# Value stage: left operands listed one product earlier, four buffers for V's outputs, block stores begun by ScalarE, one tile's scaling on GpSimd

## The chip, the cores and the metric

The kernel runs on one core of one Trainium2 chip. The metric is device time in microseconds (us) of one execution, from three executions of the kernel, of which the median is taken; a fourth execution was run under the profiler, and every row of the profile comes from that one. Engines carry the profile's names: PE is TensorE (matmul), DVE is VectorE, ACT is ScalarE, POOL is GpSimd and SP is SyncE, which in this kernel only begins DMA transfers.

## The reference

The computation is a two-layer trunk over 2048 rows of 1024 channels. The first layer is a chunked gMLP mixer; the second is banded attention that reads a K and a V computed once from the rows after the first layer. What matters here is the V half of that shared projection:

```python
def rms_norm(x, g):
    xf = x.astype(jnp.float32)
    y = xf * lax.rsqrt(jnp.mean(xf * xf, axis=-1, keepdims=True) + EPS)
    return (y * g.astype(jnp.float32)).astype(x.dtype)

def shared_kv(x, g_kv, w_kv):
    bsz, s, _ = x.shape
    k, v = jnp.split(rms_norm(x, g_kv) @ w_kv, 2, axis=-1)
...
    x = x + gmlp_mixer(...)                     # layer A
    k_pad, v_pad = shared_kv(x, kv_norm_g, w_kv)
    h = rms_norm(x, b_norm_g[i])
    x = x + chunk_attention_mixer(h, k_pad, v_pad, b_w_qz[i], b_rel_bias[i], b_w_out[i])
    return rms_norm(x, final_norm_g)
```

All of it is float32. The kernel writes each float32 operand of a matmul as the sum of a high part (a cast to the type fp32r) and a low part (the operand less its high part), and forms a product as hi·hi + hi·lo + lo·hi: three matmuls instead of one.

## The kernel before, in words

**Stages.** Layer A runs until about 1347 us of the span. Then comes the *Value stage* (to about 1520 us), which computes V for all 2048 rows, and then, tile by tile, the projections to K, Q and Z (tile names `pj`, `raw_b`, `wh_b`, `wl_b`), attention (`s`, `tp`, `pv`) and the output projection.

**The Value stage.** It takes the rows in four tiles t = 0 to 3 of 512 rows, each four blocks b = 0 to 3 of 128 rows. The V product of a tile (512x1024 by 1024x1024) is done by Strassen's scheme with seven half-size products, taken in the order ph = 1, 7, 2, 6, 5, 4, 3 (`PHS`), each for two halves of the rows, jp = 0, 1. I write (ph,jp) for one of these fourteen products of a tile. A product is twelve matmuls into one PSUM tile: for each k = 0 to 3 one hi·hi (L111), one high left by low weight (L112), one low left by high weight (L113). Three kinds of work stand around the matmuls:

- *Left operands* (`v_left`, L1257 to L1280). For each product ACT casts a 128x512 part of the normalised rows to its high part `Shv` (L337) and DVE subtracts it for the low part `Slv` (L342). Then, in place, POOL forms the sums of Strassen's scheme: after ph = 1 `a11 -= a21` (L1273) and `a21 += a22` (L1274), after ph = 7 `a11 = a22 - a11` (L1276), after ph = 2 `a12 -= a11` (L1278). Block buffers of even tiles are named `bx_b`, those of odd tiles `xo_b`; blocks 0 and 1 hold the operands of jp = 0, blocks 2 and 3 those of jp = 1. PE's L113 of a product waits for its `Slv`.
- *Eviction* (`v_evict`, L1288 to L1326). DVE combines the products (L1314, L1317, L1319, L1322, L1325), POOL adds two of them (L1320), and a finished 128x512 part of V is split again into a buffer `v` by ACT (L1296) and DVE (L1297), and stored to DRAM by SP (L1301, `vhd<-v`). The buffers `v` are two.
- *Next tile's rows.* While tile t is multiplied, `norm(t+1,b)` loads a block (L141), sums its squares on ACT (L143), adds epsilon on DVE (L125), raises to -1/2 on POOL (L126, `rr_b`) and scales the block on DVE (L148). `block(t+1,b)` then transposes it on PE (L162, eight 128x128 transposes into two PSUM banks of four), ACT copies the result back (two L168), and SP stores it to DRAM for later (L169, `xtd<-xo_b` or `xtd<-bx_b`). POOL's sums overwrite the block in place, so the first of them must wait for that store to have landed.

In tile 0 the weights of the later products are split as well (ACT L228, DVE L229: `vwh`, `vwl`), because they are loaded there for the first time.

**What sets the order.** `strassen()` (L296) is a generator: it writes out the matmuls of a product, yields four times per product, and asks for the left operands of a later product (`ready`) and for weights (`weigh`) after the second k. The loop over tiles (L1336 on) uses the yields, numbered i = 0 to 55 in a tile, to write out `norm` and `block` of the next tile (for t = 0 from i = 30 and i = 45 every 3; otherwise from i = 1 every 3 and i = 20 every 8). The framework's scheduler then gives every engine its list, near to that written order; an engine works through its list strictly in order and waits on semaphores. What is written earlier is therefore ahead in the list of each engine it touches.

Of the kernel before, what the change touches and what calls it, by code (L numbers as in the profile page):

```python
# [10 lines left out]
F32R = mybir.dt.float32r  # L11
BF16 = mybir.dt.bfloat16
AF = mybir.ActivationFunctionType
ALU = mybir.AluOpType
# [3 lines left out]
P = 128  # L18
# [4 lines left out]
NT = S // T  # L23
# [10 lines left out]
def trunk_kernel(  # L34
# [19 lines left out]
    nc = tc.nc  # L54
# [84 lines left out]
    def norm(t, b, junk):  # L139
        xt = xf[t, b] = place[0](t, b)  # L140
        nc.sync.dma_start(xt[:], x1d[t][b * P : (b + 1) * P, :])  # L141
        r = sm.tile([P, 1], F32, tag="rr", name=f"rr_b{t}_{b}", bufs=4)
        on_tick(nc.scalar.activation(  # L143
            junk(f"jk_b{t}_{b}")[:].bitcast(BF16), xt[:], AF.Square, scale=1.0 / 32,
            accum_out=r[:],
        ))
        root(r[:])
        nc.vector.tensor_scalar(xt[:], xt[:], r[:], None, op0=ALU.mult)  # L148

    def x_tiles():  # L150
        th = sh.tile([P, KD, T], F32R, tag="hh", name="hh_b")
# [3 lines left out]
    def block(t, b):  # L155
        xt = xf[t, b]
        half = [
            banks[0].tile([P, 4, P], F32, tag="t4", name=f"tr_b{t}_{b}_{h}", bufs=4)
            for h in range(2)
        ]  # L160
        for k in range(KD):
            ins = tpose(half[k // 4][:, k % 4, :], xt[:, k * P : (k + 1) * P], ident[:])  # L162
            if k == 0:
                on_tick(ins)
        x3 = xt[:].rearrange("p (k c) -> p k c", k=KD)
        for h in range(2):
            ks = slice(h * 4, h * 4 + 4)
            nc.scalar.copy(x3[:, ks, :], half[h][:])  # L168
        nc.sync.dma_start(xtd[t][:, b, :], xt[:])  # L169

    x_place = []

# [118 lines left out]

    PHS = (1, 7, 2, 6, 5, 4, 3)

    def strassen(name, right, left, evict, look):

        todo = [(ph, jp) for ph in PHS for jp in range(2)]  # L296
        rts, views = {}, {}

        def weigh(n):
            for ph in PHS[:n]:  # L300
                if ph not in rts:
                    rts[ph] = right(ph)

        def ready(i):
            if i < len(todo):
                views[i] = left(*todo[i])

        ready(0)
        if not look:
            yield  # L310
        weigh(1)
        deep = look == 2
        if deep:
            ready(1)
        for i, (ph, jp) in enumerate(todo):
            ps = pmm.tile([P, 512], F32, tag="mm", name=f"{name}_{ph}_{jp}")
            vs = views.pop(i)
            for k in range(4):
                hi, lo = rts[ph][k // 2]
                c = slice((k % 2) * 512, (k % 2) * 512 + 512)  # L320
                ins = mm3(ps[:], *vs[k], hi[:, c], lo[:, c], k == 0, k == 3)
                tick.append(ins.ins.name)
                if k == 1:
                    weigh(i // 2 + (2 if jp else 1 + look))
                    ready(i + 1 + deep)
                if k < 3:
                    yield
            evict(ph, jp, ps[:])
            yield
# [54 lines left out]
    with ExitStack() as actx:  # L384
# [624 lines left out]
        for n in range(2, 6):  # L1009
            b = start[n, 1]  # L1010
# [219 lines left out]
    with ExitStack() as vctx:  # L1230
        def v_pool(name):
            return vctx.enter_context(tc.tile_pool(name=name, bufs=1, reuse_waits="tile"))

        def v_weights(pool, ph):
            for q in range(2):
                vw[ph, q] = [pool.tile([P, 1024], F32R, name=f"vw{i}{ph}_{q}")[:] for i in "hl"]

        vpw, vps, vpx, vpc, vpu, vpv, vpy, vp2, vpt = (
            v_pool(n) for n in ("vpw", "vps", "vpx", "vpc", "vpu", "vpv", "vpy", "vp2", "vpt")
        )  # L1240
        for ph in (4, 3):
            v_weights(vpw, ph)
# [45 lines left out]
        def v_evict(t):  # L1288
            xa, ya = {}, {}

            def out(r, c, jp, y):
                v = vpv.tile([P, 4, 256], F32R, tag="v", name=f"v{t}_{r}{c}{jp}", bufs=2)
                o4 = y.rearrange("p (a b c) -> p a b c", a=4, b=2)
                for hd in range(2):
                    h = v[:, :, hd * 192 : hd * 192 + 64]
                    nc.scalar.copy(h, o4[:, :, hd, :])  # L1296
# [4 lines left out]
                nc.sync.dma_start(  # L1301
                    vhd[t][:, 4 * c : 4 * c + 4, 2 * jp + r, :], v[:].bitcast(F32)
                )
# [28 lines left out]
        )  # L1332
        pieces = []
        vsplit = []
        for t in range(NT):
            for i, _ in enumerate(  # L1336
                strassen(f"vp{t}", v_right(t), v_left(t), v_evict(t), 1 if t else 2)
            ):
                n0, b0 = (30, 45) if t == 0 else (1, 20)
                dn, db = (3, 3) if t == 0 else (3, 8)  # L1340
                if i and i % 4 == 0 and vsplit:
# [18 lines left out]

# [705 lines left out]
```

## Time and profile before

| what | before |
|---|---|
| median of 3 executions | 2645.97 us (2645.60 to 2647.23) |
| profiled execution: time / span | 2649.25 us / 2647.5 us (1.75 us lie around the span) |
| mean granted PE clock | 0.997 |
| busy: PE, DVE, ACT, POOL | 98%, 71%, 49%, 34% |
| PE waits in the stretch 1340 to 1530 us, by the table of waits | 8.1 us in 9 waits |

How to read it: PE is busy in all but 2% of the span and works strictly in order, so time is lost only where PE waits, and a wait taken out there moves everything behind it forward. The table of waits lists, for one engine, the line it waited at, the engine and line that released it, the sum, how often and the longest. In the timeline each row is a start, a duration, the engine, the line, the operation with out<-in names, and in brackets the idle time before it and what ended that; `x2` marks neighbouring like rows put together. SP's rows are the issue of a transfer, not the transfer itself; the view of one tile gives the time from issue to landing.

### The profile page before, as it was taken

How to read it: one execution, taken by the hardware profiler on the slowest of the kernel's cores; microseconds unless marked ns; L12 is line 12 of the kernel's file. 1: busy time of each engine (PE TensorE's matmuls, PEld its weight loads, DVE VectorE, ACT ScalarE, POOL GpSimd, SP SyncE). 2: the span in 40 equal slices, each digit the busy share in tenths (PEclk: the TensorE clock that was granted, in tenths of full speed). 3: DMA queues.
4: the chain of work that ended last, by engine and by line, in shares of the span. 5: the costliest groups of instructions: out<-in, count | busy, mean ns of one | idle time of the engine just before them, and what ended most of it. 6: DMA issues, size and time to landing. Idle time of an engine off the chain costs nothing. (4 is left out here: it accounts for less than half of the span.)

```text
span 2647.5 us, 38028 instructions
## 1 busy us (share of the span) xinstructions
PE 2607.3 (98%) x12976; PEld 2179.8 (82%) x12976; DVE 1889.1 (71%) x2946; ACT 1303.1 (49%) x2303; POOL 893.7 (34%) x874
## 2 busy tenths in 40 slices
PE   8999999999999999999999999999999999999997
PEld 7888888888888888888878778888888888888886
DVE  6655676766767668757777767778778777877677
ACT  5422243443433434343356456666666655666564
POOL 4611335143152322203234434344332232332245
PEclk9999999999999999999999999999999999999999
DMA  7898998989988868967776587778787666875666
GB/s 291 313 347 331 345 367 321 315 324 340 335 318 294 311 235 328 328 201 270 282 266 209 194 284 229 233 240 264 251 269 258 224 208 220 256 229 159 195 227 249
DMA packets 273857, 718.74 MB, mean 271 GB/s; under 512 B 28800, under 2 KB 68736, under 8 KB 273664
## 3 DMA queue, kind: packets, MB, share of 16 engines
q1 hardware_dynamic: 273664, 716.31, 78.2%
q8 instruction: 104, 1.70, 0.3%
q14 instruction: 89, 0.73, 0.1%
HBM read 531.12 MB, written 174.59 MB: 267 GB/s over the span
## 5 line engine op out<-in xcount | busy, mean ns | idle before, releaser
L111 PE MATMUL P<-T,S 128*128 128x512 f32 x1248 | 495.7, 397 | 0.0
L113 PE MATMUL P<-T,S 128*128 128x512 f32 x1248 | 488.1, 391 | 0.1
L112 PE MATMUL P<-T,S 128*128 128x512 f32 x1248 | 487.8, 391 | 0.2 <-DVE T L444 0.2
L1488 POOL TENSOR_SCALAR pr<-pr,sl 128x640 f32<-128x640 f32 (+4 forms) x256 | 206.9, 808 | 553.9 <-DVE sl L1487 467.4
L111 PE MATMUL pj<-hh_b,wh_b 128*128 128x512 f32 x768 | 319.9, 417 | 0.7 <-ACT wh_b L228 0.7
L113 PE MATMUL pj<-hh_b,wl_b 128*128 128x512 f32 x768 | 304.2, 396 | 0.8 <-DVE wl_b L229 0.7
L112 PE MATMUL pj<-hl_b,wh_b 128*128 128x512 f32 x768 | 302.9, 394 | 0.1
L1484 ACT ACTIVATE pr<-pr,nm 128x640 f32<-128x640 f32 (+4 forms) x256 | 195.5, 764 | 186.2 <-DVE nm L1477 184.8
L113 PEld LDWEIGHTS P<-T,S 128*128 128x128 f32 x1248 | 234.6, 188 | 50.9 <-DVE S L444 0.4
L112 PEld LDWEIGHTS P<-T,S 128*128 128x128 f32 x1248 | 235.3, 189 | 45.3 <-DVE T L444 0.6
L111 PEld LDWEIGHTS P<-T,S 128*128 128x128 f32 x1248 | 235.2, 188 | 44.8 <-DVE x L577 0.4
L1509 DVE TENSOR_TENSOR pt<-tp,pt 128x640 fp32r<-128x640 f32 (+4 forms) x256 | 188.5, 736 | 43.8 <-ACT pt L1508 41.2
L1477 DVE CUSTOM_DVE_ANT_0 pr<-s,bias 128x640 f32<-128x640 f32 (+4 forms) x256 | 188.1, 735 | 32.5 <-PE s L1469 27.2
L1508 ACT CAST pt<-tp 128x640 fp32r<-128x640 f32 (+4 forms) x256 | 159.0, 621 | 54.1 <-PE tp L1504 49.7
L1504 PE MATMUL tp<-ident,pr 128*128 128x128 f32 x1120 | 166.5, 274 | 9.6 <-DVE pt L1509 7.8
L113 PEld LDWEIGHTS pj<-hh_b,wl_b 128*128 128x128 f32 x768 | 144.4, 188 | 35.7 <-DVE wl_b L229 2.9
L1504 PEld LDWEIGHTS tp<-ident,pr 128*128 128x128 f32 x1120 | 130.6, 140 | 44.3 <-issue 14.6
L111 PEld LDWEIGHTS pj<-hh_b,wh_b 128*128 128x128 f32 x768 | 145.3, 189 | 18.8 <-ACT wh_b L228 2.4
L1529 PEld LDWEIGHTS pv<-pt,V 128*128 128x128 f32 x896 | 143.0, 188 | 20.2 <-DVE pt L1509 3.2
L112 PEld LDWEIGHTS pj<-hl_b,wh_b 128*128 128x128 f32 x768 | 145.3, 189 | 16.9 <-DVE hl_b L186 0.5
L1529 PE MATMUL pv<-pt,V 128*128 128x256 f32 (+3 forms) x896 | 153.9, 319 | 1.9 <-ACT pt L1508 1.0
L229 DVE TENSOR_TENSOR wl_b<-raw_b,wh_b 128x1024 fp32r<-128x1024 f32 x96 | 120.2, 1253 | 28.2 <-ACT wh_b L228 27.0
(302 smaller groups left out, 5732.7 us busy)
## 6 DMA issues: line engine op xcount, KB each, us to landing
S<-hsd SPq DMA_DIRECT2D x288, 512.0 KB, 5.5
rw<-in_w_a SPq DMA_DIRECT2D x108, 512.0 KB, 6.5
A<-ytd SPq DMA_DIRECT2D x72, 512.0 KB, 5.8
raw_b<-wk SPq DMA_DIRECT2D x72, 512.0 KB, 4.3
hsd<-S SPq DMA_DIRECT2D x56, 512.0 KB, 4.7
V<-vhd SPq DMA_DIRECT2D x56, 512.0 KB, 5.6
bias<-reld SPq DMA_DIRECT2D x64, 320.0 KB, 3.9
va<-vd SPq DMA_DIRECT2D x32, 512.0 KB, 6.0
```

Of the source, the lines that this page charges most:

```text
L111: first = mm(ps, lh, rh, start=first, stop=False)
L112: mm(ps, lh, rl, start=False, stop=False)
L113: mm(ps, ll, rh, start=False, stop=last)
L229: tv(wl[:], raw[:], wh[:].bitcast(F32), op=sub)
L1477: nc.vector.tensor_tensor_reduce(out=pr[:, c0:].rearrange("p (a b) -> p a b", a=nseg), in0=ps[:, :nseg, :w], in1=bias[:, c0:].rearrange("p ...
L1484: nc.scalar.activation(pr[:, c0:], pr[:, c0:], AF.Exp, scale=-1.0, bias=nm[:], accum_out=sl[:])
L1488: nc.gpsimd.tensor_scalar(pr[:, c0:], pr[:, c0:], sl[:], 1.0, op0=ALU.mult, op1=ALU.mult)
L1504: ins = tpose(tp[:, b, :], pr[:, b * P : (b + 1) * P], ident[:])
L1508: nc.scalar.copy(oh, tp[:, b0:5, :].rearrange("p a b -> p (a b)"))
L1509: nc.vector.tensor_tensor(pt[:, 2560 + o + b0 * P : 2560 + o + 640], tp[:, b0:5, :].rearrange("p a b -> p (a b)"), oh.bitcast(F32), op=ALU ...
L1529: mm(po[:, q0 * P : q1 * P], vtl[t, p][:, i, hs], rhs, start=(i == blocks[0] and j == 0), stop=(i == 7 and j == 1),)
```

## The change

It has four parts.

1. *Left operands listed further ahead.* `strassen()` takes `deep`, and lists the operands of `deep` + 1 products before the first matmul, and then always of the product `deep` + 1 ahead: three ahead in tile 0 (was two), two ahead in tiles 1 to 3 (was one). The generators of all tiles are made beforehand, and the next tile's is started at i = 54 of the current tile, so that the operands of its first products are listed before the current tile's last eviction.
2. *Four buffers for V's outputs.* The parts of V with c = 1 (`v_010`, `v_011`, `v_110`, `v_111`) get a pool of their own, `vpz`, with two buffers; those with c = 0 keep `vpv`.
3. *Block stores begun by ScalarE.* `xtd<-xo_b` and `xtd<-bx_b` go from SP's list to ACT's.
4. *One scaling on GpSimd.* `norm` of tile 1 (which runs during tile 0) scales its four blocks on POOL instead of DVE.

The diff:

```diff
@@ norm
-        nc.vector.tensor_scalar(xt[:], xt[:], r[:], None, op0=ALU.mult)
+        if t == 1:
+            nc.gpsimd.tensor_scalar(xt[:], xt[:], r[:], 1.0, op0=ALU.mult, op1=ALU.mult)
+        else:
+            nc.vector.tensor_scalar(xt[:], xt[:], r[:], None, op0=ALU.mult)
@@ block
-        nc.sync.dma_start(xtd[t][:, b, :], xt[:])
+        nc.scalar.dma_start(xtd[t][:, b, :], xt[:])
@@ strassen
-    def strassen(name, right, left, evict, look):
+    def strassen(name, right, left, evict, look, deep=0):
...
         ready(0)
-        if not look:
+        for i in range(deep):
+            ready(i + 1)
+        if deep or not look:
             yield
         weigh(1)
-        deep = look == 2
-        if deep:
-            ready(1)
         for i, (ph, jp) in enumerate(todo):
...
                     ready(i + 1 + deep)
@@ v_evict
-                v = vpv.tile([P, 4, 256], F32R, tag="v", name=f"v{t}_{r}{c}{jp}", bufs=2)
+                pool = vpz if c else vpv
+                v = pool.tile([P, 4, 256], F32R, tag="v", name=f"v{t}_{r}{c}{jp}", bufs=2)
@@ the loop over tiles
+        tiles = [
+            strassen(f"vp{t}", v_right(t), v_left(t), v_evict(t), 1 if t else 2, 1 if t else 2)
+            for t in range(NT)
+        ]
+        next(tiles[0])
         for t in range(NT):
-            for i, _ in enumerate(
-                strassen(f"vp{t}", v_right(t), v_left(t), v_evict(t), 1 if t else 2)
-            ):
+            for i, _ in enumerate(tiles[t]):
...
+                if i == 54 and t + 1 < NT:
+                    next(tiles[t + 1])
```

Added lines shift the line numbers a little: in the changed kernel `Slv` is L344, POOL's four sums are L1276, L1277, L1279 and L1281, the evictions L1318 to L1329, DVE's scaling L151 and POOL's L149, the block store L172.

PE's list is the same but for one group of transposes that moves by one matmul, and the lists of DVE and POOL in tiles 2 and 3 are unchanged. The instructions move at three places.

**DVE in tile 0, from the split of the first weights of ph = 4 on** (`vw` are weights, `Slv_4_0` is the left operand of product (4,0), `rr_b_0` and `xo_b_0` belong to block 0 of tile 1). Before:

```order
L229 TENSOR_TENSOR vwl_0_11952<-st_0_12142,vwh_0_11951 128x1024
L125 TENSOR_SCALAR rr_b_0_12176<-rr_b_0_12176 128x1
L1319 TENSOR_TENSOR vu_1_1_12017<-vp_6_1_12158,vu_1_1_12017 128x512
L148 TENSOR_SCALAR xo_b_0_12174<-xo_b_0_12174,rr_b_0_12176 128x1024
L229 TENSOR_TENSOR vwl_1_11954<-st_1_12144,vwh_1_11953 128x1024
L342 TENSOR_TENSOR Slv_4_0_12201<-bx_b_1_11687,Shv_4_0_12200 128x512
L125 TENSOR_SCALAR rr_b_1_12206<-rr_b_1_12206 128x1
```

and now:

```order
L232 TENSOR_TENSOR vwl_0_11955<-st_0_12149,vwh_0_11954 128x1024
L344 TENSOR_TENSOR Slv_4_0_12175<-bx_b_1_11687,Shv_4_0_12174 128x512
L125 TENSOR_SCALAR rr_b_0_12183<-rr_b_0_12183 128x1
L1323 TENSOR_TENSOR vu_1_1_12025<-vp_6_1_12165,vu_1_1_12025 128x512
L232 TENSOR_TENSOR vwl_1_11957<-st_1_12151,vwh_1_11956 128x1024
L344 TENSOR_TENSOR Slv_4_1_12208<-bx_b_3_11828,Shv_4_1_12207 128x512
L125 TENSOR_SCALAR rr_b_1_12213<-rr_b_1_12213 128x1
```

`Slv_4_0` now stands right behind the first weight split, four rows earlier; the scaling L148 is gone from DVE's list, and `Slv_4_1` has come up to where `rr_b_1` was.

**POOL at the turn from tile 0 to tile 1** (`xo_b` are tile 1's blocks, `rr_b_0_12434`, now `rr_b_0_12442`, and `rr_b_1` the norm of tile 2). Before:

```order
L1273 TENSOR_TENSOR xo_b_0_12174<-xo_b_0_12174,xo_b_1_12204 128x512
L1276 TENSOR_TENSOR xo_b_0_12174<-xo_b_1_12204,xo_b_0_12174 128x512
L1274 TENSOR_TENSOR xo_b_1_12204<-xo_b_1_12204 128x512
L126 TENSOR_TENSOR rr_b_0_12434<-rr_b_0_12434,mhalf 128x1
L126 TENSOR_TENSOR rr_b_1_12454<-rr_b_1_12454,mhalf 128x1
L1273 TENSOR_TENSOR xo_b_2_12233<-xo_b_2_12233,xo_b_3_12263 128x512
L1274 TENSOR_TENSOR xo_b_3_12263<-xo_b_3_12263 128x512
```

and now:

```order
L1276 TENSOR_TENSOR xo_b_0_12181<-xo_b_0_12181,xo_b_1_12211 128x512
L1277 TENSOR_TENSOR xo_b_1_12211<-xo_b_1_12211 128x512
L1276 TENSOR_TENSOR xo_b_2_12240<-xo_b_2_12240,xo_b_3_12270 128x512
L1279 TENSOR_TENSOR xo_b_0_12181<-xo_b_1_12211,xo_b_0_12181 128x512
L1277 TENSOR_TENSOR xo_b_3_12270<-xo_b_3_12270 128x512
L126 TENSOR_TENSOR rr_b_0_12442<-rr_b_0_12442,mhalf 128x1
L126 TENSOR_TENSOR rr_b_1_12462<-rr_b_1_12462,mhalf 128x1
```

The sums on blocks 2 and 3, which need the stores of these two blocks, have moved ahead of the two powers of tile 2's norm.

**DVE at the same turn**, from the first norm of tile 2 on. Before, with `Slv_7_1` (the left operand of tile 1's fourth product) as the last row:

```order
L125 TENSOR_SCALAR rr_b_0_12434<-rr_b_0_12434 128x1
L148 TENSOR_SCALAR bx_b_0_12432<-bx_b_0_12432,rr_b_0_12434 128x1024
L1297 TENSOR_TENSOR v_011_12407<-vu_1_1_12017,v_011_12407 128x4x64 x2
L125 TENSOR_SCALAR rr_b_1_12454<-rr_b_1_12454 128x1
L148 TENSOR_SCALAR bx_b_1_12452<-bx_b_1_12452,rr_b_1_12454 128x1024
L342 TENSOR_TENSOR Slv_7_1_12492<-xo_b_2_12233,Shv_7_1_12491 128x512
L342 TENSOR_TENSOR Slv_2_0_12520<-xo_b_0_12174,Shv_2_0_12519 128x512
L342 TENSOR_TENSOR Slv_2_1_12540<-xo_b_2_12233,Shv_2_1_12539 128x512
```

and now:

```order
L125 TENSOR_SCALAR rr_b_0_12442<-rr_b_0_12442 128x1
L151 TENSOR_SCALAR bx_b_0_12440<-bx_b_0_12440,rr_b_0_12442 128x1024
L125 TENSOR_SCALAR rr_b_1_12462<-rr_b_1_12462 128x1
L151 TENSOR_SCALAR bx_b_1_12460<-bx_b_1_12460,rr_b_1_12462 128x1024
L344 TENSOR_TENSOR Slv_7_1_12472<-xo_b_2_12240,Shv_7_1_12471 128x512
L125 TENSOR_SCALAR rr_b_2_12486<-rr_b_2_12486 128x1
L151 TENSOR_SCALAR bx_b_2_12484<-bx_b_2_12484,rr_b_2_12486 128x1024
L344 TENSOR_TENSOR Slv_2_0_12500<-xo_b_0_12181,Shv_2_0_12499 128x512
```

`Slv_7_1` has the two scalings of tile 2 ahead of it in both lists, and now the scaling of block 2 stands ahead of `Slv_2_0` as well. On ACT the stores of blocks 2 and 3 (L172) stand, in this order, behind the copies of block 2 and the cast `Shv_1_1`, and behind the first cast of `v_011`, tile 0's last output.

Two smaller moves concern transfers: SP's load of the raw weight `raw_b_2_1` of the projection (L246), which stood ahead of the first stores of `Qh`, now stands behind the load `V_1` of attention, and the load `raw_b_2_0` behind it.

More of the change, by code (lines that the diff above doesn't have):

```diff
@@ L1236, in v_weights @@
                 vw[ph, q] = [pool.tile([P, 1024], F32R, name=f"vw{i}{ph}_{q}")[:] for i in "hl"]
-        vpw, vps, vpx, vpc, vpu, vpv, vpy, vp2, vpt = (
-            v_pool(n) for n in ("vpw", "vps", "vpx", "vpc", "vpu", "vpv", "vpy", "vp2", "vpt")
+        vpw, vps, vpx, vpc, vpu, vpv, vpy, vp2, vpt, vpz = (
+            v_pool(n)
+            for n in ("vpw", "vps", "vpx", "vpc", "vpu", "vpv", "vpy", "vp2", "vpt", "vpz")
         )
```

## The prediction

> **What bounds the kernel now.** I read the table of PE's waits over the Value stage first, then PE's own timeline at each wait, then the engine that released it.
>
> ```profile
> engine line waited for: us in total, times, longest us
> PE vp L113 <- DVE Slv L342: 5.2, 5, 1.7
> PE vp L113 <- DVE rr_b L125: 1.4, 1, 1.4
> PE pj L111 <- ACT wh_b L228: 0.7, 1, 0.7
> PE pj L113 <- DVE wl_b L229: 0.5, 1, 0.5
> PE vp L111 <- ACT Shv L337: 0.3, 1, 0.3
> ```
>
> PE is the bound, and all that a change in this stage can win is the 8.1 us of these nine waits and the restarts behind them. PE's rows put them in four places:
>
> ```profile
> 1370.79 0.39 PE L111 MATMUL vp<-vwh,Shv 128*128 128x512 f32 x1
> ...
> 1373.51 0.39 PE L111 MATMUL vp<-vwh,Shv 128*128 128x512 f32 x1
> ...
> 1376.93 0.50 PE L113 MATMUL vp<-vwh,Slv 128*128 128x512 f32 x1 [1.45 <-DVE rr_b L125]
> ...
> 1379.56 0.39 PE L112 MATMUL vp<-vwl,Shv 128*128 128x512 f32 x1
> 1381.48 0.50 PE L113 MATMUL vp<-vwh,Slv 128*128 128x512 f32 x1 [1.53 <-DVE Slv L342]
> ...
> 1387.00 0.51 PE L113 MATMUL vp<-vwh,Slv 128*128 128x512 f32 x1 [0.94 <-DVE Slv L342]
> ...
> 1402.78 0.50 PE L111 MATMUL vp<-vw,Shv 128*128 128x512 f32 x1 [0.26 <-ACT Shv L337]
> 1404.05 0.50 PE L113 MATMUL vp<-vw,Slv 128*128 128x512 f32 x1 [0.53 <-DVE Slv L342]
> ...
> 1512.66 0.50 PE L113 MATMUL vp<-vwh,Slv 128*128 128x512 f32 x1 [0.51 <-DVE Slv L342]
> 1517.37 0.50 PE L113 MATMUL vp<-vwh,Slv 128*128 128x512 f32 x1 [1.70 <-DVE Slv L342]
> 1526.09 0.50 PE L111 MATMUL pj<-hh_b,wh_b 128*128 128x512 f32 x1 [0.72 <-ACT wh_b L228]
> ```
>
> A wait costs more than its bracket. The first two rows, the same matmul of two neighbouring products, stand 2.72 us apart: twelve matmuls at 0.227 us. L112 at 1379.56 and the L113 right behind it at 1381.48 stand 1.92 us apart, so this wait costs 1.69 us for a bracket of 1.53; I add 0.2 us to each wait. With that, the four places hold: end of tile 0, products (4,0), (4,1), (3,0): 3.92 in brackets, **4.5**; tile 1, product (7,1): 0.79, **1.3**; end of tile 3: 2.21, **2.7**; start of the projection: 1.2 (0.7 + 0.5 of the table), **1.8**. Sum 10.3 us, 0.4% of 2649.25. The table's nine waits are all in these places (the ninth is the `wl_b` just behind the last row), so tile 2, and tile 1 past its first products, have none to win.
>
> **Tile 0: operands listed earlier, scaling off DVE.** These rows carry the first wait:
>
> ```profile
> 1370.45 1.21 DVE L229 TENSOR_TENSOR vwl<-st,vwh 128x1024 fp32r<-128x1024 f32 x1
> ...
> 1373.36 1.78 DVE L148 TENSOR_SCALAR xo_b<-xo_b,rr_b 128x1024 f32<-128x1024 f32 x1 [1.04 <-POOL rr_b L126]
> 1375.06 1.21 DVE L229 TENSOR_TENSOR vwl<-st,vwh 128x1024 fp32r<-128x1024 f32 x1
> 1376.20 0.68 DVE L342 TENSOR_TENSOR Slv<-bx_b,Shv 128x512 fp32r<-128x512 f32 x1
> ```
>
> `Slv_4_0`, the last row, ends at 1376.9 and PE wanted it at 1375.33. It is late because DVE stood still for 1.04 us in front of L148, and because L148 then took 1.78. In the new list it follows the first L229, so it can be done at 1371.6 + 0.6 = 1372.2, three microseconds early. `Slv_4_1` moves past two scalings and two evictions and is early too. Both waits (1.6 and 1.7) go. From DVE's list here go also the idle time before L148, its stretch and four times its own 0.75: about 1.0 + 1.0 + 3.0 = 5 us.
>
> What is late next: PE comes 3.3 us sooner to (3,0), and `Slv_3_0` still queues behind DVE's evictions and a third L229; and PE's transposes of block 3 wait for the PSUM banks of block 1, whose copy on ACT stands behind the two casts of `v_100` and `v_101` that DVE's evictions release. And POOL now does the scaling, four times, in the same stretch:
>
> ```profile
> 1370.67 2.15 POOL L1320 TENSOR_TENSOR vu<-vu,vu 128x512 f32<-128x512 f32 x1 [9.05 <-DVE vu L1319]
> 1372.78 0.54 POOL L126 TENSOR_TENSOR rr_b<-rr_b,mhalf 128x1 f32<-128x1 f32 x1
> 1373.30 1.29 POOL L1320 TENSOR_TENSOR vu<-vu,vu 128x512 f32<-128x512 f32 x1
> ```
>
> ```profile
> L1488 POOL TENSOR_SCALAR pr<-pr,sl 128x640 f32<-128x640 f32 x192 | 171.1, 891 | 437.4 <-DVE sl L1487 391.2 <-PE s L1469 18.1 <-DVE rr_f L1809 7.4
> L213 POOL TENSOR_TENSOR raw_b<-raw_b,bg 128x1024 f32<-128x1024 f32 x16 | 31.0, 1937 | 0.0
> ```
>
> No POOL scaling of 128x1024 is in the trace; 128x640 takes 0.89, by size 1.4 us for 1024, and the two-input L213 of that size takes 1.94: I take 1.4, nearest by kind. POOL sat idle for 9.05 us before L1320, so it has the time. But the rows show the two engines holding each other: L1320 at 1370.67 took 2.15 beside L229, where its like took 1.29 at 1373.30, and beside this one L148 took 1.78, 1.03 over its undisturbed 0.75. Four scalings can so give back up to 4 x 1.0 us of the 5 us taken off DVE. My sum: the first two waits go (3.3), of the third (1.1) half stays, and a new wait of 0.5 to 2 us comes at the transposes and the last weight split. Gain **2.2 us**; ends: 0 (the port takes all) and 4.5 (no wait is left).
>
> The Trainium skill, page "Perfetto Trace Analysis", section "Optimizing Scalar/DVE Operations", says that GpSimd and VectorE share a port which a two-port VectorE operation holds as an exclusive lock, so that moving work between these two might not help. The rows above agree that they delay each other (2.15 against 1.29; 1.78 against 0.75). By the page alone the scaling would win nothing, and the sum would be that of the third rival, 2646.3.
>
> **Tile 1: the same listing puts a store in front of PE.** This is the term that goes the other way.
>
> ```profile
> 1391.61 5.12 SPq L1301 DMA_DIRECT2D vhd<-v  x2
> 1396.78 1.50 SPq L169 DMA_DIRECT2D xtd<-xo_b  x2
> ```
>
> ```profile
> 1400.75 1.33 POOL L1273 TENSOR_TENSOR xo_b<-xo_b,xo_b 128x512 f32<-128x512 f32 x1 [0.61 <-DMA xtd<-xo_b]
> 1402.16 1.28 POOL L1274 TENSOR_TENSOR xo_b<-xo_b 128x512 f32<-128x512 f32 x1
> ```
>
> ```profile
> 1398.03 0.75 DVE L148 TENSOR_SCALAR bx_b<-bx_b,rr_b 128x1024 f32<-128x1024 f32 x1 [1.04 <-POOL rr_b L126]
> ...
> 1402.76 5.24 DVE L342 TENSOR_TENSOR Slv<-xo_b,Shv 128x512 fp32r<-128x512 f32 x4 [1.83 <-ACT Shv L337]
> ```
>
> Before, the stores of blocks 2 and 3 sat on SP behind two `vhd` stores until 1396.78, so POOL's L1273 on block 2 began at 1400.75, and `Shv_7_1`, `Slv_7_1` were 1.3 us late. On ACT the stores are begun sooner, counted from the end of tile 0 (T; before 1394.16, now some 2.2 earlier): block 2 at T + 0 to 1.4, when the copies and the cast ahead of it on ACT are through; block 3, which stands behind the first cast of `v_011`, not before DVE has evicted the last product (0.7), ACT has cast (0.4) and begun the transfer (0.4), so T + 1.5, and twice that where DVE is still busy.
>
> ```profile
> L169 SPq DMA_DIRECT2D xtd<-xo_b x8: 332/477/911, 1386.9 to 1473.6; - x8
> ...
> DMA to landing us min/median/max: 2.9/4.2/7.1
> ```
>
> But POOL now does its sums on blocks 0, 2 and 3 before tile 2's two powers, and DVE's two scalings of tile 2 stand in front of `Slv_7_1`. The chain: block 3 lands at T + 1.5 to 3 + 4.2 = T + 5.7 to 7.2; L1274 1.28; power 0.54; scaling 0.75; epsilon and the second power, which follow the first scaling, 0.6; second scaling 0.75; `Slv` 0.6: T + 10.2 to 11.7. PE wants `Slv_7_1` three products and a piece after T, at T + 8.6. So PE waits 1.6 to 3.1 us there. `Slv_2_0` then needs POOL's sum on block 2, which overwrites what `Slv_7_1` read (1.3), a power (0.54), a scaling (0.75) and itself (0.6): 3.2 against PE's 2.72, 0.5 more, or 0.9 where POOL is held up; and `Slv_2_1` the same once more. Together 2.6 to 4.9, I take 4.0 with restarts, against 1.3 before: **a loss of 2.7 us**. Ends: landing at 7.1 adds 2.9, a loss of 6.5; landing at 2.9 is then limited by POOL's three sums in a row and saves little, but with ACT's list running a microsecond ahead and no restarts the loss is 0.5; a gain of 1.3 only if the wait vanishes altogether.
>
> **Projection: four buffers.** ACT's last casts of V waited for a free `v`:
>
> ```profile
> 1519.14 0.71 ACT L1296 CAST v<-vu 128x256 fp32r<-128x256 f32 x2 [1.64 <-DMA vhd<-v]
> 1521.15 0.71 ACT L1296 CAST v<-vu 128x256 fp32r<-128x256 f32 x2 [1.30 <-DMA vhd<-v]
> 1524.38 0.71 ACT L1296 CAST v<-vu 128x256 fp32r<-128x256 f32 x2 [2.52 <-DMA vhd<-v]
> 1525.00 1.99 ACT L228 CAST wh_b<-raw_b 128x1024 fp32r<-128x1024 f32 x2
> ```
>
> `wh_b` stood behind 5.5 us of such waits, and PE waited for it at 1526.09. With two more buffers the last two pairs take turns with buffers whose stores are older; only the last product's eviction remains ahead, and L228 comes at least 2 us sooner. The 1.8 us go: **gain 1.8** (ends 1.0 and 1.8). The end of tile 3 stays: DVE is held there by POOL's L213, and both lists are as before: **0** of 2.7.
>
> **Attention's start.** SP's load of `raw_b_2_1` moves back past ten stores and loads, from 1527.33 to about 1536. Its consumer on POOL stood at 1542.29:
>
> ```profile
> 1542.29 1.90 POOL L213 TENSOR_TENSOR raw_b<-raw_b,bg 128x1024 f32<-128x1024 f32 x1
> ...
> 1547.20 0.63 PE L1504 MATMUL tp<-ident,pr 128*128 128x128 f32 x4 [0.66 <-POOL pr L1488]
> ```
>
> Like loads land in 4.3 us by the page's table of issues, so at 1540.5: just in time. As PE arrives a little earlier, I take a **loss of 0.4** (0 to 1.2).
>
> **Sum.** 2.2 - 2.7 + 1.8 - 0.4 = 0.9 us gained: 2648.35 for the profiled execution, and with the 3.28 us between it and the median, **2645.1 us**. All terms lie inside the 0.2% (5.3 us) that a measurement of this kernel can tell from no change.
>
> **Rivals.**
>
> - *All waits that the change touches vanish* (4.5 + 1.3 + 1.8 = 7.6): 2638.4. For it: PE's waits are all for operands and these are listed sooner; the store is begun sooner than at 1396.78. Against: the chain at (7,1) is counted from rows, and it would have to shrink by 1.6 to 3.1 us. Two thirds of this gain (over 5.3 us) are already a measurable one. 0.25.
> - *DVE blocked at tile 1's start* (the slower side): DVE's list is strictly in order, and `Slv_7_1` to `Slv_2_1` each stand behind a scaling that waits for a power behind a sum behind a store. If the store of block 3 begins at T + 5 because `v_011`'s cast in front of it is late, and takes the longest landing of the view, 7.1, then `Slv_7_1` is ready at T + 16.6, and the waits are 8.0 there and 1.4 behind it; with tile 0's gain halved by the port: -8.1 + 1.1 + 1.8 - 1.0 = 6.2 lost, 2652.2. It decides from the point where block 3's store lands later than T + 11.2: then `Slv_7_1` is ready at T + 15.7, PE waits 7.1 there and 1.4 behind it, and the net loss passes 5.3. 0.13.
> - *The port takes tile 0's gain*: earlier listing wins only the first two waits, POOL's scalings bring 1 to 2 us of waits elsewhere: 1 - 2.7 + 1.8 - 0.4 = -0.3, 2646.3. This is no change again, and shares the 0.62 of my forecast.
>
> **How the numbers follow.** No change 0.62, measurable gain 0.25, measurable loss 0.13. The likeliest case's own range is 2641.5 to 2649.5 (tile 0's term from 0 to 4.5, tile 1's from -6.5 to -0.5, not at their worst ends together). To leave out no more than 2 in 10 on both sides, I extend it to 2639 to 2650.5.
>
> **What would show it.** Right: no wait of PE at L113 for (4,0) and (4,1); a wait of some 2 to 3 us for `Slv_7_1`, and two of half a microsecond or more behind it, DVE idle there for POOL's L126 and POOL idle for `xtd<-xo_b`; no PE wait at the projection's first L111; unchanged waits at the end of tile 3. Wrong: PE without a wait at tile 1's start (then the first rival), POOL's scaling far over 1.4 us with DVE's subtractions doubled beside it (then the third), or a wait at a place where neither list moved.

## The result and the profile after

| | before | changed |
|---|---|---|
| median of 18 executions each | 2646.35 us (2642.94 to 2652.07) | 2652.07 us (2648.53 to 2658.22) |
| ratio to before, 95% interval | | 1.0018 (1.0011 to 1.0024) |
| profiled execution: time / span | 2649.25 / 2647.5 us | 2648.61 / 2646.8 us |

The change makes the kernel slower by 0.18%, 4.8 us (2.9 to 6.4). That is clear of zero, just inside the 0.2% that I had called no change, and the median lies above my range. The two profiled executions alone would mislead: the changed one is the shorter. Why, stands at the end of this section.

The table of PE's waits over the same stretch and the start of attention (1340 to 1550 us), changed kernel:

```profile
PE vp L113 <- DVE rr_b L125: 4.4, 1, 4.4
PE vp L113 <- DVE Slv L344: 2.2, 2, 1.7
PE vp L111 <- ACT Shv L339: 1.6, 1, 1.6
PE tp L1513 <- POOL pr L1497: 1.6, 1, 1.6
PE tr_b L165 <- ACT xo_b L171: 1.6, 1, 1.6
```

Of the waits before, the three at the end of tile 0 and the two of the projection are gone, and those at the end of tile 3 (2.2 in two) stand unchanged. New are 1.6 us at a group of transposes in tile 0, and 6.0 us at tile 1's product (7,1); the wait at attention's first `tp` grew from 0.7 to 1.6 us. PE's timeline gives their places, and what follows the longest:

```profile
1388.85 1.06 PE L165 MATMUL tr_b<-ident,xo_b 128*128 128x128 f32 x8 [1.56 <-ACT xo_b L171]
...
1400.46 0.50 PE L111 MATMUL vp<-vw,Shv 128*128 128x512 f32 x1 [1.62 <-ACT Shv L339]
1400.80 0.39 PE L112 MATMUL vp<-vw,Shv 128*128 128x512 f32 x1
1405.63 0.80 PE L113 MATMUL vp<-vw,Slv 128*128 128x512 f32 x1 [4.44 <-DVE rr_b L125]
1406.23 0.63 PE L111 MATMUL vp<-vw,Shv 128*128 128x512 f32 x1
1406.66 0.63 PE L112 MATMUL vp<-vw,Shv 128*128 128x512 f32 x1
```

After the wait the matmuls take 0.63 us instead of 0.39 and start 0.43 us apart instead of 0.227, until 1409.64. The windows of the changed kernel show why (columns: window, its length, busy us of PE, PEld, DVE, ACT and POOL with instructions, granted PE clock, share of the DMA engines, GB/s):

```profile
1400.00:1404.00 4.00, 0.73 (x2) 0.30 (x2) 0.81 (x2) 4.00 (x9) 3.07 (x4) 0.87 0.52 181
1404.00:1408.00 4.00, 2.37 (x6) 1.88 (x7) 1.94 (x4) 0.49 (x1) 1.97 (x3) 0.50 0.00 0
```

The granted clock was 0.50 there. Ten matmuls at 0.43 instead of 0.227 cost 2.0 us on top of the waits.

To see where time went I compare stretches between the same matmuls on PE: from the first matmul of a tile to that of the next, then to the first `tp` row and the first `pv` row after it. The last column is the change's difference.

| stretch | before, us | changed, us | difference |
|---|---|---|---|
| tile 0 | 46.61 | 43.63 | -2.98 |
| tile 1 | 43.05 | 50.27 | +7.22 |
| tiles 2 and 3 | 82.54 | 82.54 | 0.00 |
| projection, to the first `tp` | 19.78 | 17.92 | -1.86 |
| attention, to the first `pv` | 9.17 | 10.12 | +0.95 |
| sum | 201.15 | 204.48 | +3.33 |

So tile 1 takes back more than the other parts win. That the changed profile is still 0.7 us shorter over its whole span has mostly to do with the clock elsewhere. The windows of the kernel before show two stretches with half a clock that the changed one lacks:

```profile
48.00:52.00 4.00, 2.88 (x13) 2.41 (x14) 3.36 (x6) 0.59 (x1) 3.40 (x3) 0.75 0.70 270
52.00:56.00 4.00, 4.00 (x16) 3.26 (x15) 0.69 (x1) 0.59 (x1) 0.43 (x1) 0.82 0.97 313
1584.00:1588.00 4.00, 3.55 (x15) 2.80 (x15) 3.18 (x9) 1.72 (x5) 2.28 (x3) 0.75 0.60 153
1588.00:1592.00 4.00, 4.00 (x18) 3.29 (x17) 2.48 (x5) 1.56 (x4) 0.75 (x2) 0.82 0.70 192
```

The shortfall of the clock is (0.25 + 0.18) x 4 = 1.7 us in each, so PE lost some 3.4 us there, and the changed execution had the clock at 1.00 in the same windows, with PE busy for about as long (2.76 and 4.00, 3.55 and 4.00). That makes up for the 3.33 us of the table; the remaining 0.6 us lie elsewhere and were not followed. Over all thirteen profiles of this study the first of these drops is there in ten and the second in three; they come and go between executions, and only many executions average them out.

### The profile page after: what moved, and what is told of

Its sections match the earlier page's. It is cut to its first block, busy times and chain, and to the rows that moved or that the text cites. A ratio compares the mean times of both kernels' runs of the same rounds, so it can differ in the third digit from the quotient of the medians.

```text
span 2646.8 us, 38010 instructions
## 1 busy us (share of the span) xinstructions
PE 2605.2 (98%) x12976; PEld 2179.4 (82%) x12976; DVE 1884.7 (71%) x2942; ACT 1302.0 (49%) x2303; POOL 901.3 (34%) x878
## 4 chain that ended last, share of the span: by engine, by line
PE 81%; DVE 7%; DMA 5%; issue 2%; POOL 2%; ACT 1%; SPq 1%; DVEq 0%; POOLq 0%; ACTq 0%
PE P L111 11%; PE P L113 11%; PE P L112 11%; PE pj L113 6%; PE pj L111 6%; PE pj L112 6%; PE pv L1538 5%; PE s L1478 4%; PE tp L1513 4%; PE Po L113 2%; PE Po L112 2%; PE Po L111 2%; DMA A<-ytd 1%; PE vp L113 1%; PE vp L112 1%
## 5 line engine op out<-in xcount | busy, mean ns | idle before, releaser
L113 PE MATMUL P<-T,S 128*128 128x512 f32 x1248 | 487.5, 391 | 0.0
L113 PE MATMUL pj<-hh_b,wl_b 128*128 128x512 f32 x768 | 303.8, 396 | 0.4 <-DVE wl_b L232 0.3
L113 PEld LDWEIGHTS P<-T,S 128*128 128x128 f32 x1248 | 234.3, 188 | 50.9 <-DVE S L446 0.4
L113 PEld LDWEIGHTS pj<-hh_b,wl_b 128*128 128x128 f32 x768 | 144.1, 188 | 34.5 <-DVE wl_b L232 2.0
```

The costliest lines, as they stand in the source:

```text
L113: mm(ps, ll, rh, start=False, stop=last)
```

## The experiments

The theory I went in with, A: the loss is the chain in front of `Slv_7_1` (block store, POOL's sums, power, scaling, DVE's strict order), made longer because tile 2's norm stands inside it. Rivals: B, stores begun by ACT land late, and that alone is the loss; C, the scaling on POOL. All runs were timed against the kernel before in five rounds.

**Tile 2's norm listed later.**

```diff
-                n0, b0 = (30, 45) if t == 0 else (1, 20)
+                n0, b0 = (30, 45) if t == 0 else (12, 20)
```

> The change with one edit: in tiles 1 and 2 the next tile's norm is listed from i = 12 on instead of i = 1. Theory A (the loss of tile 1 is DVE's Slv_7_1 standing behind the scalings of tile 2, which stand behind powers, sums and block stores; with a clock drop after the long wait): the 4.4 us wait at (7,1) falls under 1 us, the 1.6 us wait for Shv stays since the sum on block 2 still needs its store, the clock stays at 1.00; counted from the stage's start, tile 1 costs 1 to 2.5 us more than before instead of 7.2, and the whole comes out 4 to 5 us below the change, at 0.998 to 1.000 of the kernel before. Rival B (the block stores begun by ACT land late and that alone makes PE wait): the wait at (7,1) stays at 4 us or more, 1.0018. Rival C (the scaling on POOL does it): no difference from the change, 1.0018.

Ratio 1.0006 (0.9997 to 1.0015), median 2648.43. PE at tile 1, and the clock behind it:

```profile
1399.16 0.50 PE L111 MATMUL vp<-vw,Shv 128*128 128x512 f32 x1 [1.60 <-ACT Shv L339]
1400.29 0.50 PE L113 MATMUL vp<-vw,Slv 128*128 128x512 f32 x1 [0.40 <-DVE Slv L344]
```

```profile
1398.00:1402.00 4.00, 2.44 (x8) 1.69 (x9) 2.86 (x3) 3.51 (x7) 4.00 (x4) 0.89 0.78 272
1402.00:1406.00 4.00, 4.00 (x14) 3.16 (x13) 3.38 (x3) 3.46 (x7) 4.00 (x3) 0.68 0.01 5
```

The 4.4 us wait went to 0.4 by this line alone; the wait for `Shv` stayed at 1.6, as it should, since POOL's sum on block 2 still needs its store. Tile 1 costs 3.07 us more than before instead of 7.22. I expected 1 to 2.5, a full clock and a ratio of at most 1.000; the clock still halved, after waits of only 1.6 and 0.4 us. So the norm's place is most of tile 1's loss, 4.15 of 7.22 us, but not all. Attention's start took 11.90 us instead of the change's 10.12: its first `tp` waited 3.4 us instead of 1.6, though SP's list is the same. Why it waited longer was not followed.

**Block stores back on SP.**

```diff
-        nc.scalar.dma_start(xtd[t][:, b, :], xt[:])
+        nc.sync.dma_start(xtd[t][:, b, :], xt[:])
```

> The change with the block stores given back to SP. Theory A: the stores of blocks 2 and 3 are begun later, behind two stores of V, so the chain in front of Slv_7_1 gets longer: the wait at (7,1) is 6 to 10 us, the result 2 to 4 us above the change, 1.0025 to 1.0035 of the kernel before. Rival B (ACT's stores are the cause): back to the kernel before or better, 0.998 to 1.000. Rival C: as the change, 1.0018.

Ratio 1.0000 (0.9992 to 1.0009), median 2646.96. Here theory A was wrong: the stores came no later, and landed sooner. The time is the one that rival B forecast, but the run doesn't prove B, as POOL's rows will show. SP and POOL in this kernel:

```profile
1388.88 0.46 SPq L172 DMA_DIRECT2D xtd<-xo_b  x1
1390.26 0.36 SPq L1305 DMA_DIRECT2D vhd<-v  x1
1390.72 2.34 SPq L172 DMA_DIRECT2D xtd<-xo_b  x2
...
1398.28 1.61 SPq L179 DMA_DIRECT2D xr_b<-xtd  x2
```

```profile
1394.73 0.55 POOL L126 TENSOR_TENSOR rr_b<-rr_b,mhalf 128x1 f32<-128x1 f32 x1
1395.97 1.57 POOL L1276 TENSOR_TENSOR xo_b<-xo_b,xo_b 128x512 f32<-128x512 f32 x1 [0.69 <-DMA xtd<-xo_b]
```

The stores of blocks 2 and 3 are begun at 1390.72, and POOL starts on block 2 at 1395.97, 5.3 us later. In the changed kernel ACT began block 2's store at 1391.31 and POOL started at 1398.49, 7.2 us later. There SP, rid of the block stores, had begun the reloads of tile 0's rows at the same moment:

```profile
1389.16 0.86 SPq L179 DMA_DIRECT2D xr_b<-xtd  x1
1390.82 0.52 SPq L1305 DMA_DIRECT2D vhd<-v  x1
1391.39 1.51 SPq L179 DMA_DIRECT2D xr_b<-xtd  x1
```

Tile 0 was also 1.9 us shorter with SP's stores (41.75): the 1.56 us wait at the transposes is gone, because in ACT's list the copy of block 1 stands between the casts of `v_100` and `v_101` again instead of behind both. With the waits of 1.32 and 1.98 us at (7,1) and a clock drop, tile 1 took 47.20. The edit moved more than the stores, however: in POOL's list the first power of tile 2's norm (1394.73) now stands ahead of the sum on block 2, where the changed kernel has both powers behind the last sum (1402.17), so DVE's first scaling no longer waits for block 2's store. Landing and order can't be told apart by this run. That late stores alone are not the loss follows from the run before, where they stayed on ACT and the 4.4 us went.

**Scaling back on DVE.**

```diff
-        if t == 1:
-            nc.gpsimd.tensor_scalar(xt[:], xt[:], r[:], 1.0, op0=ALU.mult, op1=ALU.mult)
-        else:
-            nc.vector.tensor_scalar(xt[:], xt[:], r[:], None, op0=ALU.mult)
+        nc.vector.tensor_scalar(xt[:], xt[:], r[:], None, op0=ALU.mult)
```

> The change with the four scalings of tile 1's norm given back to DVE. Theory A: the loss at tile 1's start stays (5 to 8 us in the profile); in tile 0 the gain of 3 us shrinks to between 0 and 2, since DVE gets 3 us of work back; 1.0018 to 1.0030. Rival C: back to the kernel before or better, 0.998 to 1.000. Rival B: as the change, 1.0018.

Ratio 1.0013 (1.0004 to 1.0021), median 2651.79. Tile 0 took 45.59 instead of 43.63: PE now waited for a weight split behind DVE's scalings,

```profile
1385.00 0.50 PE L112 MATMUL vp<-vwl,Shv 128*128 128x512 f32 x1 [1.19 <-DVE vwl L229]
```

and the wait at the transposes was gone. The wait of 4.4 us at (7,1) stayed, but the one for `Shv` ahead of it was gone, so tile 1, 48.38, was 1.9 us shorter than in the change. A wait for `Shv` stands instead at tile 1's first matmul, which belongs to tile 0's stretch:

```profile
1392.31 0.50 PE L111 MATMUL vp<-vw,Shv 128*128 128x512 f32 x1 [1.36 <-ACT Shv L336]
```

Tiles 0 and 1 together take 93.97 us, against 93.90 in the change, so in the change the move to POOL wins nothing that the sum shows. The ratio is below the 1.0018 to 1.0030 that I expected and close to the change's. Rival C falls: without the scaling on POOL the loss is still there.

**Longer listing in tile 0 alone.**

```diff
-            strassen(f"vp{t}", v_right(t), v_left(t), v_evict(t), 1 if t else 2, 1 if t else 2)
+            strassen(f"vp{t}", v_right(t), v_left(t), v_evict(t), 1 if t else 2, 0 if t else 2)
...
-                if i == 54 and t + 1 < NT:
-                    next(tiles[t + 1])
```

> The change with the longer listing in tile 0 alone: tiles 1 to 3 list one product ahead as before, and no generator is started early. Theory A: two of the powers of tile 2 come before POOL's last sums again, but the scaling of block 2 now stands in front of Slv_7_1, so part of the wait stays: 1 to 4 us at (7,1), no clock drop; the gain in tile 0 (3 us) and at the projection (1.8 us) stays; 0.9985 to 1.0005. Rivals B and C: as the change, 1.0018.

Ratio 1.0024 (1.0015 to 1.0033), median 2653.40: a miss. I had blamed the listing across tiles for putting the norm in front; without it the wait was longer, 5.4 us, and tile 1 took 51.34. It also came one product earlier, at (7,0), the third product behind tile 1's first matmul at 1390.44:

```profile
1404.41 0.79 PE L113 MATMUL vp<-vw,Slv 128*128 128x512 f32 x1 [5.38 <-DVE rr_b L125]
```

```profile
1400.59 0.76 DVE L151 TENSOR_SCALAR bx_b<-bx_b,rr_b 128x1024 f32<-128x1024 f32 x1 [3.84 <-POOL rr_b L126]
...
1403.00 0.75 DVE L151 TENSOR_SCALAR bx_b<-bx_b,rr_b 128x1024 f32<-128x1024 f32 x1 [1.60 <-POOL rr_b L126]
1403.67 0.68 DVE L344 TENSOR_TENSOR Slv<-xo_b,Shv 128x512 fp32r<-128x512 f32 x1
```

The last row, the third `Slv` of the tile, is `Slv_7_0`. Listed only one product ahead, it stands behind the two scalings of tile 2 already, and `Slv_7_1` behind a third. The listing across tiles is not the cause; where tile 2's norm stands is.

**Reloads held back.** To separate "ACT's stores are slow" from "they now run beside SP's reloads", the stores stay on ACT and the four reloads are tied to tile 3, where they are written:

```diff
-        nc.sync.dma_start(
+        ld = nc.sync.dma_start(
             xt[:].rearrange("p (b c) -> p b c", b=TB), xtd[t][:, :, cs]
         )
+        if t == 0:
+            on_tick(ld)
```

> The change with one edit: the four reloads xr_b<-xtd of tile 0, which SP may begin during tile 0 since the block stores left its list, are tied to the product of tile 3 beside which they are written, so none runs during the turn from tile 0 to tile 1. Theory D (ACT's block stores land late because SP's reloads now run beside them on the same DMA engines): the longest landing of xtd<-xo_b falls from 10.9 us to 7 or less, the store of block 2 is in within 5.5 us instead of 7.2, PE's wait for Shv (1.6) goes to 0.5 or less and the wait at (7,1) from 4.4 to 2.5 to 3.5 us; 2 to 3 us below the change, 1.0004 to 1.0012 of the kernel before. Rival E (stores begun by ACT are slow by themselves): landings and waits as in the change, 1.0018.

Ratio 1.0003 (0.9994 to 1.0011), median 2649.49. POOL and PE:

```profile
1397.08 1.28 POOL L1278 TENSOR_TENSOR xo_b<-xo_b,xo_b 128x512 f32<-128x512 f32 x1 [1.38 <-DMA xtd<-xo_b]
```

```profile
1399.07 0.50 PE L111 MATMUL vp<-vw,Shv 128*128 128x512 f32 x1 [0.20 <-ACT Shv L341]
1404.26 0.79 PE L113 MATMUL vp<-vw,Slv 128*128 128x512 f32 x1 [4.46 <-DVE rr_b L125]
```

ACT began this store at 1391.39, so POOL started 5.7 us after it, and PE's wait for `Shv` fell from 1.62 to 0.20. The reloads beside the stores are so worth about 1.5 us of landing, which speaks for theory D. (The 10.9 us that I named is the landing of a reload, which the view of the tile `xtd` counts among the stores; tile 1's stores took at most 7.0 us from issue to landing in the change and 5.5 here.) But the wait at L113 stayed at 4.5, where I expected 2.5 to 3.5: PE only came to it earlier. Tile 1 took 48.80, 1.5 us less than in the change.

**Both mended: stores on SP and norm from i = 12** (the two diffs above).

> The change with the block stores on SP and the next tile's norm listed from i = 12 on in tiles 1 and 2. If the two losses found so far are separate (the norm in front of Slv_7_1, and the landing of the stores), both go: at tile 1 one wait for Shv of about 1.3 us stays and the wait at L113 falls from 2.0 us to 0.4 or less; counted from the stage's start tile 1 costs 2 to 3 us less than with SP's stores alone; 0.9985 to 0.9995 of the kernel before, with the wait of attention's first tp at 1.6 us or more. If the norm's place matters only where the stores are late, no better than 1.0000.

Ratio 0.9983 (0.9975 to 0.9992), median 2644.18: faster than the kernel before. Tile 0 took 41.75 and tile 1 44.36; the waits at (7,1) are 0.78 and 0.52, and the clock stays full. I had expected some 1.3 and at most 0.4. Attention's start, however, took 12.81 instead of 9.17, with a wait of 3.0 us at `tp` and a clock drop behind it (0.57 in 1544 to 1548).

**The same with the new pool allocated first.**

```diff
-        vpw, vps, vpx, vpc, vpu, vpv, vpy, vp2, vpt, vpz = (
+        vpz, vpw, vps, vpx, vpc, vpu, vpv, vpy, vp2, vpt = (
             v_pool(n)
-            for n in ("vpw", "vps", "vpx", "vpc", "vpu", "vpv", "vpy", "vp2", "vpt", "vpz")
+            for n in ("vpz", "vpw", "vps", "vpx", "vpc", "vpu", "vpv", "vpy", "vp2", "vpt")
```

> The same, with the new pool of two buffers allocated ahead of the other eight instead of behind them. Theory F (the late load raw_b_2_1 comes from where the new pool lies in memory: its buffer's place is free only after the last stores of V): SP's load stands ahead of the stores of Qh again, and the wait of the first tp for POOL falls from 1.6 to 3.4 us to under 1 us; 1 to 2 us below the kernel without it, 0.998 to 0.999 of the kernel before. Rival (the wait of tp has another cause): as without it.

Ratio 0.9974 (0.9965 to 0.9984), median 2642.26: the best so far, and a little more than expected. SP's load of `raw_b_2_1` stands ahead of the stores of `Qh` again, and the first `tp` waits 0.64 us as before:

```profile
PE vp L113 <- DVE Slv L344: 2.7, 3, 1.7
PE vp L111 <- ACT Shv L339: 0.7, 1, 0.7
PE tp L1513 <- POOL pr L1497: 0.6, 1, 0.6
PE tr_b L165 <- DVE rr_b L125: 0.6, 1, 0.6
```

Attention's start took 9.18. Against the kernel without this edit the intervals overlap, so the time alone doesn't separate the two; the wait in the profile does, and it is back at 0.6 to 0.7 us in all four profiles with this edit.

**Four buffers alone, in the kernel before.**

```diff
-                v = vpv.tile([P, 4, 256], F32R, tag="v", name=f"v{t}_{r}{c}{jp}", bufs=2)
+                pool = vpz if c else vpv
+                v = pool.tile([P, 4, 256], F32R, tag="v", name=f"v{t}_{r}{c}{jp}", bufs=2)
```

> The kernel before with the four buffers for V's outputs alone. Theory A: nothing changes in tiles 0 to 3; the two waits at the projection's start (1.8 us) go; the load raw_b_2_1 comes later, so the first tp waits 1 to 2 us instead of 0.7; net 0.5 to 1.5 us gained, 0.9994 to 0.9998. If the buffers win also inside the stage: 0.999 or less.

Ratio 1.0000 (0.9991 to 1.0009). The profile is as expected: projection 17.93 instead of 19.78, attention's start 10.25 instead of 9.17, the tiles within 0.2 us. Over all stretches 0.6 us are won, which is below what five rounds can tell.

**Each part in the mended kernel.** Last, three parts undone one at a time in the mended kernel, where no long wait stands in the way. The edits are those above: stores on ACT, scaling on DVE, listing across tiles off.

> The mended kernel (stores on SP, norm from i = 12, new pool allocated first) with the block stores given back to ACT, nothing else. If the stores on ACT cost by themselves, by the copy of block 1 that comes behind the casts (1.9 us in tile 0) and by the later landing at tile 1: counted from the stage's start tile 0 ends 1.9 us later, tile 1 costs 2 to 3.5 us more, with a clock drop where the two waits at (7,1) add up to 2 us; 4 to 5 us above the mended kernel, 0.9985 to 1.0000 of the kernel before. If the norm's place had been the whole of the loss: within 1 us of the mended kernel, 0.9974.

> The mended kernel with tile 1's four scalings on DVE again. By the profile of the change with this part undone: tile 0 loses 2 us of its gain (PE waits for weight splits behind DVE's scalings), tile 1 as in the mended kernel; 1.5 to 2.5 us above it, 0.998 to 0.9985 of the kernel before. If the shared port takes what the move wins: within 0.5 us of the mended kernel.

> The mended kernel with the longer listing in tile 0 alone (tiles 1 to 3 one product ahead, no generator started early). By the run that undid it in the change, the listing across tiles isn't what cost; with the norm out of the way it should win little: 0 to 1.5 us above the mended kernel, 0.9974 to 0.9982. If listing further ahead is itself the loss: below the mended kernel.

| kernel | ratio (95%) | tile 0 | tile 1 | projection | attention start |
|---|---|---|---|---|---|
| mended | 0.9974 (0.9965 to 0.9984) | 41.76 | 44.31 | 18.07 | 9.18 |
| stores on ACT | 0.9993 (0.9984 to 1.0002) | 43.63 | 45.74 | 17.93 | 9.16 |
| scaling on DVE | 0.9991 (0.9982 to 0.9999) | 43.72 | 44.89 | 17.93 | 9.17 |
| one product ahead in tiles 1 to 3 | 0.9974 (0.9963 to 0.9984) | 41.75 | 44.60 | 17.93 | 9.18 |

The mended kernel's ratio comes from an earlier set of rounds than the other three. Stores on ACT cost 1.9 us in tile 0 (the copy of block 1 behind the casts) and 1.4 in tile 1, less than the 2 to 3.5 I expected there. At (7,1) they cost only 0.2: the waits were 1.10 and 0.40 instead of 0.74 and 0.53, and the clock stayed full. Most of the 1.4 is a longer wait at the first transposes of tile 2's rows, 1.67 instead of 0.59 us:

```profile
1408.73 1.06 PE L165 MATMUL tr_b<-ident,bx_b 128*128 128x128 f32 x8 [1.67 <-DVE rr_b L125]
```

The scaling on POOL is worth 2.0 us in tile 0 and 0.6 in tile 1 by the profile. The ratios stand 0.0017 apart, 4.5 us, more than the 1.5 to 2.5 I expected, but their intervals overlap. The listing across tiles is worth 0.3 us in the profile, nothing that a time shows.

## Why the prediction was wrong, step by step

- **Tile 0, gain 2.2 predicted: 2.98 measured.** Right in mechanism too: the waits of (4,0) and (4,1) went, that of (3,0) as well (I had kept half of it), and the new wait that I put at "the transposes of block 3", behind a copy that queues after the casts, is there with 1.56 us (predicted 0.5 to 2). That it needs the stores on ACT I had not seen: with SP's stores all of it is gone (it is gone too with the scaling on DVE).
- **The port.** I took 1.4 us for a scaling on POOL, nearest by kind. It took 1.13 undisturbed and 1.94 held up, in the changed kernel:

```profile
1380.63 1.13 POOL L149 TENSOR_SCALAR xo_b<-xo_b,rr_b 128x1024 f32<-128x1024 f32 x1
...
1384.67 1.94 POOL L149 TENSOR_SCALAR xo_b<-xo_b,rr_b 128x1024 f32<-128x1024 f32 x1
```

  The engines do delay each other, but in the mended kernel, where nothing else hides it, the move won 2.5 us by the profile. There the third rival, that the port takes the gain, falls. In the change the move won nothing over tiles 0 and 1 together (93.90 against 93.97 us), because other waits took the place of those it removed; whether the port has a share in that isn't shown. The Trainium skill, page "Perfetto Trace Analysis", section "Optimizing Scalar/DVE Operations", warns that such a move might not help; in the mended kernel it did. In the kernel before POOL was busy for only 6.9 of the 26 us from 1364 to 1390, and with the scaling on DVE PE waited for DVE's weight splits (1.19 us above).
- **Tile 1, loss 2.7 predicted (0.5 to 6.5): 7.22 measured.** This is the step that failed, by its size: the waits, put at 4.0 us with restarts, came to 6.5, and the clock, put at nothing, cost 2.0, which together is the 4.5 us by which the term missed. The chain was the right one and its fixed part right, 4.5 us predicted from L1274 to the end of `Slv_7_1`. In the changed kernel it is these rows of POOL and DVE, from 1400.95 to 1405.6, 4.6 us:

```profile
1398.49 1.27 POOL L1276 TENSOR_TENSOR xo_b<-xo_b,xo_b 128x512 f32<-128x512 f32 x1 [1.24 <-DMA xtd<-xo_b]
1399.72 1.27 POOL L1279 TENSOR_TENSOR xo_b<-xo_b,xo_b 128x512 f32<-128x512 f32 x1
1400.95 1.26 POOL L1277 TENSOR_TENSOR xo_b<-xo_b 128x512 f32<-128x512 f32 x1
1402.17 0.54 POOL L126 TENSOR_TENSOR rr_b<-rr_b,mhalf 128x1 f32<-128x1 f32 x1
```

```profile
1402.75 0.75 DVE L151 TENSOR_SCALAR bx_b<-bx_b,rr_b 128x1024 f32<-128x1024 f32 x1 [6.13 <-POOL rr_b L126]
...
1404.23 0.75 DVE L151 TENSOR_SCALAR bx_b<-bx_b,rr_b 128x1024 f32<-128x1024 f32 x1 [0.66 <-POOL rr_b L126]
1404.89 0.68 DVE L344 TENSOR_TENSOR Slv<-xo_b,Shv 128x512 fp32r<-128x512 f32 x1
```

  Two terms were mis-sized. First, the landing: I took the median of 4.2 us, from transfers that SP began one behind another. Block 2's store took 7.0, and POOL started 7.2 us after its issue, because the same edit let SP begin its reloads beside it; holding these back took 1.5 us off. And I let block 3's store decide, while it was block 2's, T + 8.0, with POOL's two sums behind it in a row, so that L1277 began at T + 10.5 (T = 1390.45, tile 1's first matmul) instead of T + 5.7 to 7.2. Block 3's store would hardly have let it begin sooner: it was issued at 1394.09, T + 3.6, instead of T + 1.5 to 3, took 6.4 us and landed at T + 10.0. Second, the clock, which stands nowhere in my sum: 2.0 us. The two waits of half a microsecond at (2,0) and (2,1) did not come, since PE itself was slow: at 0.227 us a matmul it would have wanted `Slv_2_0` at 1408.4, and that was ready at 1408.8; at half clock it came for it at 1410.4. Waits of 6.06 and their restarts of about 0.4, less the 1.3 of before, and 2.0 for the clock make 7.2, the 7.22 of the table.
- **Projection 1.8: 1.86. End of tile 3, no change: 0.00.** Right, and the run with the four buffers alone shows the cause of the first (1.85).
- **Attention's start, loss 0.4 (0 to 1.2): 0.95.** Inside its ends. What I called a load that "moves back" comes from where the new pool lies in memory; allocated first, it stayed in its place.
- **The slower rival** had the right place and engines, and its point of decision, `Slv_7_1` ready at T + 15.7, was nearly reached (T + 15.1), though by block 2's store and the row of sums; block 3's store, issued at T + 3.6 and not T + 5, landed at T + 10.0, half a microsecond before it was needed. I gave it 0.13, so that its price, 2652.2, lay outside my range, which ended at 2650.5. That this price stands beside the measured 2652.07 is luck: it holds 9.4 us of waits instead of 6.1 and half of tile 0's gain, and nothing for the clock.
- **The first rival**, that all three groups of waits vanish (2638.4), is what the mended kernel comes near: -5.3 us in its profile and 2642.26 in time. It took three edits that the change doesn't have, one of which takes its third part back.

## What to carry to other kernels

Taking transfers off a queue lets those behind them start earlier, so that both are under way at once; a landing time read from the old order doesn't hold for the new one (4.2 us taken, 7.0 measured, 5.5 with the reloads held back). Before listing one operand earlier on an in-order engine, follow what else is listed at that point: here the next tile's norm, moved 11 yields later, was worth 4.2 us of tile 1, and the listing across tiles 0.3. And waits of PE that come close together have to be priced with the half clock that may follow, here 2.0 us.

## What the runs showed of the hardware

The granted PE clock fell to 0.50 after waits much shorter than I had thought could matter, and the length of a single wait doesn't decide it. It halved after waits of 1.60 and 0.40 us 1.1 us apart (norm listed later), and after 1.32 and 1.98; it stayed full after 1.10 and 0.40 (mended, stores on ACT), after 0.78 and 0.52, after single waits of 1.56 to 1.70, and even after the single wait of 3.4 us at `tp` (norm listed later). In the windows of the norm run the clock's shortfall adds up to 0.44 + 1.28 = 1.7 us, that is 3.4 us at half clock; in the changed kernel 0.52 + 2.0 + 0.9, 6.8 us, twice that:

```profile
1408.00:1412.00 4.00, 4.00 (x16) 3.21 (x15) 2.09 (x5) 1.63 (x3) 1.79 (x2) 0.78 0.00 0
```

Within one execution the drops also start a whole number of such lengths apart: in the kernel before at 50.02 and 1586.02, 1536.00 us or 450 lengths of 3.413. Measured along this grid, the norm run shows what goes with a drop:

```profile
1397.73:1401.14 3.41, 1.58 (x6) 1.02 (x7) 2.00 (x2) 2.65 (x6) 3.41 (x3) 1.00 0.94 328
1401.14:1404.55 3.41, 3.41 (x10) 2.64 (x9) 3.41 (x3) 2.87 (x7) 3.41 (x3) 0.50 0.08 27
...
1541.09:1544.50 3.41, 1.71 (x8) 1.08 (x7) 0.22 (x1) 1.30 (x3) 2.57 (x2) 1.00 0.58 191
1544.50:1547.92 3.42, 1.74 (x10) 1.57 (x11) 3.36 (x10) 2.48 (x8) 1.05 (x4) 1.00 0.75 250
```

PE was busy for 1.58 us of the window ahead of the drop; the 3.4 us wait at `tp` falls across two windows, which keep 1.71 and 1.74 us each, and the clock stayed full. Between 30 and 2620 us of the thirteen profiles there are 23 such windows at half clock. Ahead of 21 of them PE was busy for at most 1.66 us of the window, ahead of the other two, near 1586, for 2.00 and 1.88; only one other window with as little (1.47 at 1548.13, reloads held back) was not followed by a drop. So in these runs a drop goes with a window in which PE idles for about half, and where the waits fall on the grid matters. No run moved a wait along the grid to test it.

The Trainium skill, page "TensorE: Matmul & The Clock Gate", section "What's actually happening", describes a gate that passes half the pulses and decides by free-running windows of about 3.4 us; the 0.50, the lengths of 3.4 and 6.8 us and the grid agree. The Trainium skill, page "TensorE: Matmul & The Clock Gate", section "Why this matters for your kernels", asks to avoid idle gaps over about 3 us; here two waits of 2.0 us together were enough, one of 3.4 was not, and the measurement decides.
